# Router fed from raw rows, first gather begun with the first tile, x loaded first and later issues in a decoder layer's mixer

## The chip, the cores and the metric

The kernel runs on one core of a Trainium2 chip. The metric is device time in microseconds (us) of one execution. PE is TensorE, PEld its weight load, DVE is VectorE, ACT is ScalarE, POOL is GpSimd, SP is SyncE (here it only issues DMAs).

## What is computed

One layer of a decoder trunk on 256 tokens of width 1024, in fp32. Cut to what matters here:

```python
# 1 token mixer: one input projection feeds three causal mixers (gated DeltaNet, RG-LRU, window attention)
y = (g_a * y_a + g_b * y_b + g_c * y_c) @ w_out
x = LN1(alpha * x + y)                                   # gain ln1_g, offset ln1_b
# 2 channel mixer: top 4 of 32 experts
logits = x @ router_w + router_b
gates = softmax(top_k(logits, 4))
# each expert: clamped SwiGLU, 1024 -> 2 x 1024 -> 1024; its weights are 12.6 MB
x = LN2(alpha * x + sum_k gates[k] * expert[idx[k]](x))
# 3 per-layer embedding
x = LN3(alpha * x + sigmoid(x @ Wg) * (p @ Wp))
```

Nothing is dropped: every token reaches its four experts.

## The kernel before

**Mixer.** The weight matrices are cut into 117 pieces of 512 KB. `load` brings a piece on SP's queue into one of four buffers `w`; `split` makes of it a high part (ACT, L423) and a low part (DVE L426 and POOL L428), in a ring of three places, `HI` and `LO`; then PE multiplies (three products for each pair of parts, L367 and L377). `run` goes over the *units* (a unit is one piece's products, or some of them) by the index u: first the evacuation of the unit before, then loads and splits, then the unit's products, then one step of every *strand*. A strand is a generator (`evac_ab`, `decays`, `inverse`, `attend`, `bias_parts`, `router` and so on) that issues some instructions and gives way with `yield`; so one `yield` puts what follows behind another unit's products in the order of every engine. `events` says which strand may go on. Each engine works in the order of issue.

**End of the mixer.** The output projection is eight units (list at L1294). `out_unit` names (tile t of 128 tokens, half c of the columns, piece kp). Its first halves read the ring, its second halves read `xh`, `xl`, `RV` and `KT`. `evac` adds the residual into `xs` (L1153) and takes statistics; `first_norm` scales and shifts the rows on DVE (L1174, L1177), transposes them (L1186) and multiplies them with the router weights (L1192). `router` then works on tile 0 and tile 1 in turn, when both have been normalised: top four, softmax, and the seat of each token in each expert by a matmul with a triangle (L1223 to L1232).

**Experts.** `group` makes one-hot matrices of the seats (L1456) and gathers the tokens of two experts by matmul (`gathered`, L1448). `expert` multiplies with the up weights (L1485; 64 seats), applies SwiGLU, multiplies with the down weights (L1520); `spread` puts the result back to the tokens (L1545) and adds it into `Y` (L1556; the first one brings the residual, L1553). The weights come on SP's queue (L1375 up, L1387 down) into a ring of ten buffers of 2 MB: four (`F`) lie apart and are filled from the mixer on (`prefetch`, L1112), six (`wq`) lie where the mixer's tiles were. Such a buffer is loaded once the mixer's tiles under it have had their last use. One expert takes four buffers for up and two for down weights. The expert pools lie one behind the other in the order in which they are opened, and so do the mixer's.

Of the kernel before, what the change touches and what calls it, by code (L numbers as in the profile page):

```python
# [18 lines left out]
D = 1024  # L19
# [6 lines left out]
SLOTS = 64  # L26
NR = T // SLOTS - 1
# [56 lines left out]
class Routing:  # L84


    def __init__(self, pl):
# [6 lines left out]
        tail = pl.tile([P, 100], F32, name="tail")  # L94
        self.ex, self.sel, self.sm, self.counts = tail[:, 0:NE], tail[:, NE:2 * NE], tail[:, 64:66], tail[0:1, 68:68 + NE]

    def softmax(self, dve, t, ex, sel, sm):

        dve.tensor_tensor_reduce(out=ex, in0=ex, in1=sel, op0=ALU.mult, op1=ALU.add, scale=1.0, scalar=0.0, accum_out=sm)
        dve.reciprocal(sm, sm)  # L100
        dve.tensor_scalar(self.G[:, t], ex, sm, None, op0=ALU.mult)

# [9 lines left out]
def mixer(mx, tc, nc, a, xs, rt, dram, cst, ones, el):  # L112
# [80 lines left out]
    warm = mp.tile([P, 1], F32, name="warm")  # L193
    pool.memset(warm, 0.0)
# [6 lines left out]
    stB = m2.tile([65, P], F32, name="stB", tag="sq")  # L201
# [6 lines left out]
    def late_parameters():  # L208
# [11 lines left out]
        pool.dma_start(rw, a["router_w"][0].rearrange("(p k) e -> p k e", k=KD))  # L220
# [4 lines left out]
    def bias_parts():  # L225
# [20 lines left out]
    pool.memset(ones, 1.0)  # L246
# [7 lines left out]
    pr = mp.tile([P, 72], F32, name="pr")  # L254
# [21 lines left out]
    def softplus(dst, src, n, neg):  # L276
# [21 lines left out]
    def parameters():  # L298
        ps = yield from banks.take()
        pe.transpose(ps[:, :65], stB, ident[:65, :65])  # L300
        dve.tensor_copy(pr[:, :65], ps[:, :65])
# [276 lines left out]
    def evac_ab(ps):  # L578
# [19 lines left out]
        yield  # L598
        p2 = yield from banks.take()
# [59 lines left out]
    def decays():  # L659

        yield from wait("G")
        dts = []
# [45 lines left out]
    def inverse():  # L708
# [272 lines left out]
    def attend(gq, qT):  # L981
# [146 lines left out]

    def norm_rows():
        while cur[0] < S + 2:  # L1130
            yield
        M["gb"] = big("TG", [P, 2, D])
        for i, n in enumerate(("ln1_g", "ln1_b")):
            act.dma_start(M["gb"][:, i], a[n].to_broadcast([P, D]))
        M["xT"] = big("MG", [P, KD, T])

    out_ps = {}

    def out_unit(work, done):
# [10 lines left out]
        def evac(_):  # L1150
            for t, c in done:
                xv = xs[:, t, halves[c]]
                dve.scalar_tensor_tensor(xv, xv, 2.0 * ALPHA, out_ps[t, c], ALU.mult, ALU.add)  # L1153
                dve.bn_stats(lns[:, t, c], xv)
                if c == 0 and t == 0:
# [3 lines left out]
                    pool.memset(M["wk"][:, 0:80], -3.0e38)  # L1159
                if c:  # L1160
# [6 lines left out]

    def first_norm(t):

        xT, gb = M["xT"], M["gb"]  # L1170
        xc = wp.tile([P, KD * P], F32, name="xc", tag="w")
        for hf in range(2):
            c = slice(hf * 512, (hf + 1) * 512)
            dve.scalar_tensor_tensor(xc[:, c], xs[:, t, c], mv[:, t, 0:1], gb[:, 0, c], ALU.subtract, ALU.mult)  # L1174
        qk = lambda v, hf: v.rearrange("p (k q) -> p q k", q=KD)[:, 4 * hf:4 * hf + 4]
# [3 lines left out]
        if t == 0:  # L1179
            yield  # L1180
        else:
            events.add("n1")
        for hf in range(2):
            b = yield from banks.take()
            for k in range(4):
                pe.transpose(b[:, k * P:(k + 1) * P], xs[:, t, (4 * hf + k) * P:(4 * hf + k + 1) * P], ident)  # L1186
            act.copy(xT[:, 4 * hf:4 * hf + 4, t * P:(t + 1) * P], b.rearrange("p (k t) -> p k t", k=4))
            banks.done(b)
        if t == 0:
            yield  # L1190
        for k in range(KD):
            pe.matmul(M["rps", t][:, :NE], xT[:, k, t * P:(t + 1) * P], rw[:, k], start=k == 0, stop=k == KD - 1)  # L1192
        events.add(f"r{t}")

    def router():

        yield from wait("r0", "n1")
# [8 lines left out]
        ex, sel = (take(NE), rt.ex), (take(NE), rt.sel)  # L1206
        m8, m4, sm = two(take(16)), two(take(16)), (take(2), rt.sm)
        posm = rt.pos
        pool.memset(m4, -3.0e38)
        for t in range(2):  # L1210
            if t:
                yield from wait("r1")
            dve.tensor_add(lg[:, t, :NE], M["rps", t][:, :NE], rb)
# [7 lines left out]
            ps2 = yield from banks.take()  # L1221
            if t == 0:
                pe.matmul(ps2[:, :NE], stri, sel[0], start=True, stop=True)  # L1223
                rt.softmax(dve, 0, ex[0], sel[0], sm[0][:, 1:2])
            else:
                pe.matmul(ps2[:, :NE], ones, sel[0], start=True, stop=False)
                pe.matmul(ps2[:, :NE], stri, sel[1], start=False, stop=True)
                pe.matmul(ps2[0:1, NE:2 * NE], ones[:, 0:1], sel[0], start=True, stop=False)
                pe.matmul(ps2[0:1, NE:2 * NE], ones[:, 0:1], sel[1], start=False, stop=True)
                act.copy(rt.counts, ps2[0:1, NE:2 * NE])  # L1230
# [588 lines left out]
```

## Time and profile before

| | |
|---|---|
| median of 3 runs | 1422.58 us (1421.93 to 1425.25) |
| the profiled execution | 1420.59 us, its span 1418.8 us |
| busy | PE 95%, DVE 42%, ACT 26%, POOL 17% |
| DMA | 481.66 MB, mean 339 GB/s |

The span is the stretch that the trace covers; the execution's own time is 1.8 us longer. A busy PE is not PE at its peak, as matmuls overlap and their ends are modelled. Times in the rows are from the span's start. A releaser ("<-") is what ended the idle time in front of an instruction.

### The profile page before, as it was taken

The page shows a single profiled execution, that of the slowest core. Times are in us where ns is not written, and L with a number is a line of the kernel's source. Part 1 is how long each engine was busy: PE and PEld are TensorE (multiplying, and loading weights), DVE is VectorE, ACT ScalarE, POOL GpSimd, SP SyncE. Part 2 cuts the span into 40 slices and gives each one's busy share as a digit, 9 for nine tenths or more (in the row PEclk, how much of TensorE's full clock was granted, in tenths as well). Part 3 has the DMA queues.
Part 4 walks back from the last instruction along what each step waited for, and adds up shares of the span by engine and source line. Part 5 has one row for each costly group of instructions (what it writes and reads, how often), then busy time and mean ns, then how long its engine had stood idle before and what let it go on. Part 6 is the DMA issues. An engine that isn't in the chain of part 4 may idle for free. (4 is left out here: it accounts for less than half of the span.)

```text
span 1418.8 us, 19330 instructions
## 1 busy us (share of the span) xinstructions
PE 1343.1 (95%) x7720; PEld 748.0 (53%) x7721; DVE 591.8 (42%) x1245; ACT 372.4 (26%) x743; POOL 247.0 (17%) x217
## 2 busy tenths in 40 slices
PE   8999989999999999999999999999999999989987
PEld 7989967888887334334333333333333333333326
DVE  6398985865565133223222222222223222222238
ACT  6767464644551111111111110111111100111122
POOL 5554864434561000000000000000000000000000
PEclk9999999999998999999999999999999999999998
DMA  9755455345888999999999999999999999999970
GB/s 264 215 137 138 133 180 168 113 135 181 307 303 339 367 427 430 428 428 426 428 429 428 428 426 429 430 428 428 426 429 430 428 427 428 429 428 428 428 296 30
DMA packets 122133, 481.66 MB, mean 339 GB/s; under 512 B 11340, under 2 KB 69340, under 8 KB 88632
## 3 DMA queue, kind: packets, MB, share of 16 engines
q1 hardware_dynamic: 120440, 477.16, 84.4%
q0 software_dynamic: 848, 1.86, 0.4%
q10 hardware_dynamic: 752, 1.38, 0.3%
q8 instruction: 62, 1.02, 0.3%
q14 instruction: 31, 0.25, 0.0%
HBM read 478.78 MB, written 3.42 MB: 340 GB/s over the span
## 5 line engine op out<-in xcount | busy, mean ns | idle before, releaser
L1485 PE MATMUL gu<-w,xe 128*64 128x512 f32 x1168 | 262.9, 598 | 6.6 <-DMA w<-in_w_gu_dram 6.6
L1485 PE MATMUL gu<-F,xe 128*64 128x512 f32 x880 | 199.2, 596 | 4.8 <-DMA F<-in_w_gu_dram 4.8
L428 POOL TENSOR_TENSOR LO<-w,HI 128x384 fp32r<-128x384 f32 (+1 forms) x113 | 168.4, 1491 | 165.9 <-ACT HI L423 154.6
L1485 PEld LDWEIGHTS gu<-w,xe 128*64 128x64 f32 x1168 | 81.7, 137 | 164.8 <-issue 144.1
L426 DVE TENSOR_TENSOR LO<-w,HI 128x640 fp32r<-128x640 f32 (+1 forms) x113 | 117.1, 1038 | 83.5 <-ACT HI L423 81.8
L1503 DVE TENSOR_SCALAR gc<-gu 128x256 f32<-128x256 f32 x64 | 26.9, 421 | 266.9 <-PE gu L1485 266.9
L1416 POOL DMA_DIRECT2D pt<-in_p_dram x1 | 0.8, 777 | 789.2 <-DVE lc L1507 789.2
L423 ACT CAST HI<-w 128x1024 fp32r<-128x1024 f32 x113 | 118.0, 1044 | 59.2 <-PE pjt L377 36.6
L1520 PE MATMUL dn<-w,hT 128*64 128x512 f32 x560 | 130.0, 607 | 2.0 <-ACT hT L1513 2.0
L1556 DVE TENSOR_TENSOR Y<-Y,cb 128x512 f32<-128x512 f32 x124 | 79.5, 682 | 116.3 <-PE cb L1545 116.3
L367 PE MATMUL pjt<-xh,HI 128*128 128x256 f32 x424 | 124.7, 294 | 0.0
L1485 PEld LDWEIGHTS gu<-F,xe 128*64 128x64 f32 x880 | 60.2, 136 | 119.0 <-issue 104.9
L367 PE MATMUL pjt<-xh,LO 128*128 128x256 f32 x424 | 120.5, 284 | 1.3 <-DVE LO L426 1.3
L367 PE MATMUL pjt<-xl,HI 128*128 128x256 f32 x424 | 120.1, 283 | 0.0
L1520 PE MATMUL dn<-F,hT 128*64 128x512 f32 x464 | 106.0, 598 | 0.0
L1504 ACT ACTIVATE sg<-gc 128x256 f32<-128x256 f32 x64 | 26.8, 419 | 286.4 <-DVE gc L1503 286.4
L1448 PE MATMUL gat<-oh,xs 128*128 128x128 f32 x512 | 76.2, 294 | 24.7 <-DVE oh L1456 19.9
L1448 PEld LDWEIGHTS gat<-oh,xs 128*128 128x128 f32 x512 | 64.4, 197 | 44.4 <-issue 27.7
L367 PEld LDWEIGHTS pjt<-xh,HI 128*128 128x128 f32 x424 | 81.5, 192 | 1.8 <-issue 1.1
L367 PEld LDWEIGHTS pjt<-xh,LO 128*128 128x128 f32 x424 | 81.3, 192 | 2.0 <-DVE LO L426 1.9
L367 PEld LDWEIGHTS pjt<-xl,HI 128*128 128x128 f32 x424 | 81.5, 192 | 0.3
L1493 DVE TENSOR_TENSOR gt<-gwt,gt 128x256 fp32r<-128x256 f32 x32 | 13.6, 424 | 152.2 <-ACT gt L1492 152.2
(404 smaller groups left out, 1713.2 us busy)
## 6 DMA issues: line engine op xcount, KB each, us to landing
w<-in_w_gu_dram SPq DMA_DIRECT2D x73, 2048.0 KB, 29.2
F<-in_w_gu_dram SPq DMA_DIRECT2D x51, 2048.0 KB, 29.4
w<-in_w_down_dram SPq DMA_DIRECT2D x70, 1024.0 KB, 19.3
F<-in_w_down_dram SPq DMA_DIRECT2D x58, 1024.0 KB, 21.0
w<-in_w_in_dram SPq DMA_DIRECT2D x85, 512.0 KB, 3.8
F<-in_w_gu_dram SPq DMA_DIRECT2D x8, 1024.0 KB, 6.8
w<-in_w_o_lru_dram SPq DMA_DIRECT2D x8, 512.0 KB, 4.7
w<-in_w_o_swa_dram SPq DMA_DIRECT2D x8, 512.0 KB, 3.8
```

What stands on the lines that cost most here:

```text
L367: pe.matmul(ps, hl[l][:, k * P:(k + 1) * P], b[r][:, k], start=k == 0 and n == 0, stop=k == KD - 1 and n == 2)
L423: act.copy(hi, s)
L426: dve.tensor_sub(lo[:, 0:n], s[:, 0:n], hi[:, 0:n].bitcast(F32))
L428: pool.tensor_tensor(out=lo[:, n:], in0=s[:, n:], in1=hi[:, n:].bitcast(F32), op=ALU.subtract)
L1416: pool.dma_start(pt, a["p"][0, 0].rearrange("(t p) c -> p t c", p=P))
L1448: pe.matmul(ps[:, kk], xs[:, t, k * P:(k + 1) * P], oh[:, t], start=t == 0, stop=t == 1)
L1485: pe.matmul(gu[64 * j:64 * j + 64, b], xe[:, k], w[:, j * D + b * 512:j * D + (b + 1) * 512], start=False, stop=k == KD - 1)
L1493: dve.tensor_sub(gt[:, 1], ps, gt[:, 0].bitcast(F32))
L1503: dve.tensor_scalar(gc[:, c], guv[:, c, 0], 7.0, None, op0=ALU.min)
L1504: act.activation(sg[:, c], gc[:, c], AF.Sigmoid, scale=1.702)
L1520: pe.matmul(dn[64 * jj:64 * jj + 64], hT[:, 2 * hf + kk, j * 64:j * 64 + 64], w[:, kk, jj * 512:(jj + 1) * 512], start=hf == j == kk == 0, ...
L1556: dve.tensor_add(y, y, pss[jj])
```

## The change

- **Order and place.** x is loaded ahead of the first weight piece, and twelve matmuls on a tile of ones run first; the first `split` comes behind the transposes of x. `evac_ab` and `decays` give way once more ahead of their matmuls, `inverse` twice more ahead of its transpose, `softplus` twice less. The `b_gu` rows are loaded on SP's queue. The attention rows are normalised on ACT.
- **Router.** Its weights are scaled by the gain beforehand (`router_weights`), and the mean's and the offset's parts are added behind (`lc_`). So the rows are transposed as they come out of the output projection, half by half (`logits`). ACT scales the rows into `xs` without gain and offset; these are applied when the gather is evacuated (`scaled_rows`) and in a separate pass for the residual (`residual`, which loads the layer-norm rows on ACT's queue).
- **Order at the end.** The output units finish tile 0 first. The router takes tile 0 by itself; its one-hot matrix and its half of the first gather come ahead of tile 1's.

```diff
+        self.oh = pl.tile([P, 2, GRP * SLOTS], F32, name="oh1")
+        self.gb = pl.tile([P, 2, KD], F32, name="gb1")
...
+    def places(self, dve, iota, t, e):
+        dve.tensor_tensor(out=self.oh[:, t].rearrange("p (e s) -> p e s", e=GRP), in0=iota[:, :SLOTS].unsqueeze(1).to_broadcast([P, GRP, SLOTS]),
+                          in1=self.pos[:, t, e:e + GRP].unsqueeze(2).to_broadcast([P, GRP, SLOTS]), op=ALU.is_equal)
+    def second(self, dve, act, pe, ps, ones, stri):
+        pe.matmul(ps[:, :NE], ones, self.sel0, start=True, stop=False)
+        pe.matmul(ps[:, :NE], stri, self.sel, start=False, stop=True)
...
+        self.seat(dve, 1, ps[:, :NE], self.sel)
+        act.copy(self.counts, ps[0:1, NE:2 * NE])
...
-                pool.dma_start(raw_b[32 * n:32 * n + 32], bsrc[g_])
+                sync.dma_start(raw_b[32 * n:32 * n + 32], bsrc[g_])
...
-            if c in (13, 9, 5):
+            if c == 9:
                 yield
...
             dve.scalar_tensor_tensor(g[:, t], g[:, t], -1.0, alog, ALU.mult, ALU.mult)
+        yield
         yield
...
         yield from wait("G")
+        yield
...
             sync.dma_start(T0[16 * b:16 * b + 16, :, c], td[b].rearrange("s i c -> i s c"))
         yield
         yield
+        yield
+        yield
...
-            dve.tensor_scalar(pr3[:, hh, 0:P], pr3[:, hh, 0:P], sm[:, 0, hh:hh + 1], None, op0=ALU.mult)
-            dve.tensor_scalar(pr3[:, hh, P:384], pr3[:, hh, P:384], sm[:, 1, hh:hh + 1], None, op0=ALU.mult)
+            act.mul(pr3[:, hh, 0:P], pr3[:, hh, 0:P], sm[:, 0, hh:hh + 1])
+            act.mul(pr3[:, hh, P:384], pr3[:, hh, P:384], sm[:, 1, hh:hh + 1])
...
+    lc_ = mpa.tile([P, 2, NE], F32, name="lc1")
...
+                if t not in rows:
+                    rows[t] = wp.tile([P, KD * P], F32, name="y", tag="w")
+                y = rows[t][:, halves[c]]
+                dve.scalar_tensor_tensor(y, xs[:, t, halves[c]], 2.0 * ALPHA, out_ps[t, c], ALU.mult, ALU.add)
...
+    def logits(t, c):
+        xT = M["xT"]
+        b = yield from banks.take()
+        for k in range(4):
+            pe.transpose(b[:, k * P:(k + 1) * P], rows[t][:, (4 * c + k) * P:(4 * c + k + 1) * P], ident)
+        act.copy(xT[:, 4 * c:4 * c + 4, t * P:(t + 1) * P], b.rearrange("p (k t) -> p k t", k=4))
+        banks.done(b)
+        yield
+        for k in range(4 * c, 4 * c + 4):
+            pe.matmul(M["rps", t][:, :NE], xT[:, k, t * P:(t + 1) * P], rw[:, k], start=k == 0, stop=k == KD - 1)
...
     def first_norm(t):
-        for hf in range(2):
-            dve.scalar_tensor_tensor(xc[:, c], xs[:, t, c], mv[:, t, 0:1], gb[:, 0, c], ALU.subtract, ALU.mult)
-        for hf in range(2):
-            dve.scalar_tensor_tensor(xs[:, t, 512 * hf:512 * hf + 512].rearrange("p (q k) -> p q k", q=4), qk(xc, hf),
-                                     mv[:, t, 2:3], qk(gb[:, 1], hf), ALU.mult, ALU.add)
+        yield
+        dve.scalar_tensor_tensor(mv[:, t, 3:4], mv[:, t, 0:1], -1.0, mv[:, t, 2:3], ALU.mult, ALU.mult)
+        for hf in range(2):
+            act.activation(xs[:, t, 512 * hf:512 * hf + 512].rearrange("p (q k) -> p q k", q=4), y[:, 4 * hf:4 * hf + 4],
+                           AF.Identity, scale=mv[:, t, 2:3], bias=mv[:, t, 3:4])
...
-    for work, done in ((both(0), ()), (both(1), ()), (second(0, 0, 1), ()), (both(2), ()), (both(3), ((0, 0), (1, 0))),
-                       (second(0, 2, 3), ((0, 1),)), (second(1, 0, 1), ()), (second(1, 2, 3), ((1, 1),))):
+    for work, done in ((both(0), ()), (both(1), ()), (second(0, 0, 1), ()), (first(0, 2, 3), ((0, 0),)),
+                       (second(0, 2, 3), ((0, 1),)), (first(1, 2, 3), ((1, 0),)), (second(1, 0, 1), ()), (second(1, 2), ()),
+                       (second(1, 3), ((1, 1),))):
...
-    load(0)
     for i in range(4):
         sync.dma_start(xs[:, :, i * 256:(i + 1) * 256], xsrc[:, :, i * 256:(i + 1) * 256])
+    load(0)
+    ps = bank(4)()
+    for _ in range(12):
+        pe.matmul(ps[:, 0:P], ones, ones, start=True, stop=True)
...
-    split(order[0][0])
     for _ in transpose_x():
         pass
+    split(order[0][0])
...
+    def scaled_rows(xe, k2, ps):
+        for kk in range(2):
+            k = 2 * k2 + kk
+            act.activation(xe[:, k], ps[:, kk], AF.Identity, scale=rt.gb[:, 0, k:k + 1], bias=rt.gb[:, 1, k:k + 1])
...
+        pss = [p1.tile([P, 2, GRP * SLOTS], F32, name="gat", tag="cb", bufs=3) for _ in range(3)]
+        pss.append(p1.tile([P, 2, GRP * SLOTS], F32, name="gat", tag="ms"))
+        for t in range(2):
+            if t:
+                rt.second(dve, act, pe, p1.tile([P, 2 * NE], F32, name="seats", tag="tr"), ones, stri)
+                rt.places(dve, iota, 1, 0)
+            for k in range(KD):
+                pe.matmul(pss[k // 2][:, k % 2], xs[:, t, k * P:(k + 1) * P], rt.oh[:, t], start=t == k % 2 == 0, stop=t == k % 2 == 1)
+                if t and k % 2:
+                    scaled_rows(xe, k // 2, pss[k // 2])
+                    yield
...
+    def residual():
+        g1, b1 = (w2.tile([P, D], F32, name=n, tag=n, bufs=1) for n in ("ob", "bd"))
+        for v, n in ((g1, "ln1_g"), (b1, "ln1_b")):
+            act.dma_start(v, a[n].to_broadcast([P, D]))
...
```

## Rows read from the trace of the kernel before

**Rows 1.** Windows: length; PE, PEld, DVE, ACT, POOL busy (instructions); PE's clock; DMA share; GB/s.
```profile
500.00:1360.00 860.00, 825.39 (x4068) 320.70 (x4065) 229.28 (x516) 100.70 (x251) 0.78 (x1) 1.00 1.01 428
```

**Rows 2.** Waits of PE, 1200 to 1370 us: total us, times, longest.
```profile
PE gu L1485 <- DMA w<-in_w_gu_dram: 4.3, 5, 1.2
```

**Rows 3.** Timeline of SP's queue: start us, us, what it issues, count.
```profile
418.57 1.85 SPq L1387 DMA_DIRECT2D w<-in_w_down_dram  x4
432.25 0.33 SPq L1375 DMA_DIRECT2D w<-in_w_gu_dram  x1
440.41 1.28 SPq L1375 DMA_DIRECT2D w<-in_w_gu_dram  x3
461.98 0.80 SPq L1387 DMA_DIRECT2D F<-in_w_down_dram  x2
```

**Rows 4.** Windows around the handover from mixer to experts.
```profile
438.00:441.00 3.00, 3.00 (x18) 2.44 (x17) 2.91 (x4) 0.19 (x1) 0.00 (x0) 1.00 0.26 109
447.00:456.00 9.00, 7.52 (x36) 6.96 (x37) 4.50 (x29) 1.41 (x5) 0.56 (x1) 0.50 1.00 430
457.00:463.00 6.00, 6.00 (x36) 2.96 (x34) 0.00 (x0) 0.74 (x2) 0.00 (x0) 1.00 0.10 14
483.00:486.00 3.00, 2.54 (x13) 0.80 (x10) 0.00 (x0) 0.37 (x1) 0.00 (x0) 1.00 0.54 137
```

**Rows 5.** Timeline of PE at the handover: start us, us, instruction, count, idle before.
```profile
417.36 0.39 PE L377 MATMUL pjt<-HI,AT 128*128 128x512 f32 x1
...
431.78 0.39 PE L377 MATMUL pjt<-LO,AT 128*128 128x512 f32 x1
...
440.17 1.14 PE L1186 MATMUL pg<-cst,xs 128*128 128x128 f32 x8
...
441.57 1.08 PE L1192 MATMUL pg<-rw,MG 128*128 128x32 f32 x8
...
453.20 3.91 PE L1448 MATMUL gat<-oh,xs 128*128 128x128 f32 x16 [0.35 <-DVE oh L1456]
457.04 1.94 PE L1485 MATMUL gu<-F,xe 128*64 128x512 f32 x8
```

**Rows 6.** Timeline of PE in the mixer, where it stood idle.
```profile
106.06 0.39 PE L600 MATMUL pg<-sc,F 128*128 128x16 f32 x2 [1.70 <-DVE sc L597]
...
112.15 2.07 PE L671 MATMUL pg<-cst,gcc 128*128 128x128 f32 x8 [1.96 <-ACT gcc L604]
121.25 1.14 PE L671 MATMUL pg<-cst,gcc 128*128 128x128 f32 x8
...
189.81 0.50 PE L377 MATMUL pjt<-LO,xh 128*128 128x512 f32 x1 [1.81 <-POOL LO L428]
...
204.19 0.50 PE L377 MATMUL pjt<-LO,xh 128*128 128x512 f32 x1 [1.47 <-DVE LO L426]
```

**Rows 7.** Timeline of POOL and of ACT around 188 us.
```profile
187.12 1.58 POOL L234 DMA_DIRECT2D rawb<-in_b_gu_dram  x3
...
190.32 0.62 ACT L240 CAST bias<-rawb 96x512 bf16<-96x512 f32 x1 [5.75 <-DMA rawb<-in_b_gu_dram]
```

**Rows 8.** Timeline of PE at the start.
```profile
5.62 1.09 PE L271 MATMUL pg<-cst,xs 128*128 128x128 f32 x4 [5.62 <-DMA xs<-in_x_dram]
...
9.79 0.36 PE L367 MATMUL pjt<-xh,HI 128*128 128x256 f32 x1
...
10.11 0.28 PE L367 MATMUL pjt<-xh,LO 128*128 128x256 f32 x1
10.23 0.28 PE L367 MATMUL pjt<-xh,HI 128*128 128x256 f32 x1
```

**Rows 9.** Groups of ACT by line: shape, count, busy us, mean ns, idle before.
```profile
L1018 ACT ACTIVATE F<-F,st 128x256 f32<-128x256 f32 x16 | 7.9, 494 | 0.0
...
L1017 ACT ACTIVATE F<-F,st 128x128 f32<-128x128 f32 x16 | 6.3, 396 | 0.1
```

**Rows 10.** Timeline of DVE at the handover.
```profile
443.72 2.21 DVE L1177 SCALAR_TENSOR_TENSOR xs<-xc,mv,TG 128x512 f32<-128x512 f32 x2
```

More of the change, by code (lines that the diff above doesn't have):

```diff
@@ L26 @@
 SLOTS = 64
+GRP = 2
 NR = T // SLOTS - 1
@@ L1127, in held_piece, with router_weights @@
         return dst
+    lc_ = mpa.tile([P, 2, NE], F32, name="lc1")
+    def router_weights():
+        yield from wait("late", "att3")
+        col = lambda i: pr[:, 65 + 8 * i:73 + 8 * i].unsqueeze(2).to_broadcast([P, KD, NE])
+        rb_ = m2.tile([P, T], F32, name="rwb", tag="sq").rearrange("p (k e) -> p k e", e=NE)
+        sums_ = m2.tile([P, T], F32, name="rws", tag="sq").rearrange("p (n e) -> p n e", e=NE)
+        dve.tensor_tensor(out=rb_, in0=rw, in1=col(1), op=ALU.mult)
+        dve.tensor_reduce(out=sums_[:, 1], in_=rb_.rearrange("p k e -> p e k"), axis=AX.X, op=ALU.add)
+        yield
+        dve.tensor_tensor(out=rw, in0=rw, in1=col(0), op=ALU.mult)
+        dve.tensor_reduce(out=sums_[:, 0], in_=rw.rearrange("p k e -> p e k"), axis=AX.X, op=ALU.add)
+        yield
+        ps = yield from banks.take()
+        pe.matmul(ps[:, 0:2 * NE], ones, sums_[:, 0:2].rearrange("p n e -> p (n e)"), start=True, stop=True)
+        yield
+        dve.tensor_scalar(lc_[:, 0], ps[:, 0:NE], -1.0, None, op0=ALU.mult)
+        dve.tensor_add(lc_[:, 1], ps[:, NE:2 * NE], rb)
+        banks.done(ps)
     def norm_rows():
@@ L1166, in out_unit @@
         return products, evac, ()
+    def logits(t, c):
[5 more added lines that the diff above has]
+        banks.done(b)
+        yield
+        for k in range(4 * c, 4 * c + 4):
+            pe.matmul(M["rps", t][:, :NE], xT[:, k, t * P:(t + 1) * P], rw[:, k], start=k == 0, stop=k == KD - 1)
+        if c:
+            events.add(f"r{t}")
     def first_norm(t):
-        xT, gb = M["xT"], M["gb"]
-        xc = wp.tile([P, KD * P], F32, name="xc", tag="w")
+        yield
+        dve.scalar_tensor_tensor(mv[:, t, 3:4], mv[:, t, 0:1], -1.0, mv[:, t, 2:3], ALU.mult, ALU.mult)
+        y = rows[t].rearrange("p (k q) -> p q k", q=KD)
         for hf in range(2):
-            c = slice(hf * 512, (hf + 1) * 512)
-            dve.scalar_tensor_tensor(xc[:, c], xs[:, t, c], mv[:, t, 0:1], gb[:, 0, c], ALU.subtract, ALU.mult)
-        qk = lambda v, hf: v.rearrange("p (k q) -> p q k", q=KD)[:, 4 * hf:4 * hf + 4]
-        for hf in range(2):
-            dve.scalar_tensor_tensor(xs[:, t, 512 * hf:512 * hf + 512].rearrange("p (q k) -> p q k", q=4), qk(xc, hf),
-                                     mv[:, t, 2:3], qk(gb[:, 1], hf), ALU.mult, ALU.add)
[L1179 to L1182, printed above, removed]
-        for hf in range(2):
[L1184 to L1193, printed above, removed]
+            act.activation(xs[:, t, 512 * hf:512 * hf + 512].rearrange("p (q k) -> p q k", q=4), y[:, 4 * hf:4 * hf + 4],
+                           AF.Identity, scale=mv[:, t, 2:3], bias=mv[:, t, 3:4])
+        events.add(f"n{t}")
     def router():
-        yield from wait("r0", "n1")
+        yield from wait("r0", "n0")
         wk = M["wk"]
@@ L1220, in router @@
             act.activation(ex[t], lg[:, t, :NE], AF.Exp, bias=sm[t][:, 0:1])
-            ps2 = yield from banks.take()
             if t == 0:
+                rt.softmax(dve, 0, ex[0], sel[0], sm[0][:, 1:2])
+                yield
+                ps2 = yield from banks.take()
                 pe.matmul(ps2[:, :NE], stri, sel[0], start=True, stop=True)
[L1224 to L1230, printed above, removed]
-            dve.scalar_tensor_tensor(posm[:, t], ps2[:, :NE], 1.0, sel[t], ALU.add, ALU.mult)
-            dve.tensor_scalar(posm[:, t], posm[:, t], -1.0, None, op0=ALU.add)
-            banks.done(ps2)
+                yield
+                rt.seat(dve, 0, ps2[:, :NE], sel[0])
+                banks.done(ps2)
+                rt.places(dve, iota, 0, 0)
     def note(name, f):
@@ L1448, in gathered @@
                     pe.matmul(ps[:, kk], xs[:, t, k * P:(k + 1) * P], oh[:, t], start=t == 0, stop=t == 1)
-            act.copy(xe[:, 2 * k2:2 * k2 + 2], ps)
+            scaled_rows(xe, k2, ps)
             yield
     def group(e):
-        oh = w2.tile([P, 2, GRP, SLOTS], F32, name="oh1", tag="oh1", bufs=1)
-        for t in range(2):
-            dve.tensor_tensor(out=oh[:, t], in0=iota[:, :SLOTS].unsqueeze(1).to_broadcast([P, GRP, SLOTS]),
-                              in1=posm[:, t, e:e + GRP].unsqueeze(2).to_broadcast([P, GRP, SLOTS]), op=ALU.is_equal)
@@ L1609, in moe @@
     gu, first = begun(0), gather
-    next(first)
-    rt.finish(dve)
+    rest = residual()
+    next(rest)
     for _ in range(2):
         next(first)
+    rt.finish(dve)
     for e in range(NE):
@@ L1621, in mid @@
                 next(first, None)
+                if k in (3, 5, 7):
+                    next(rest, None)
             if e == BIASED:
```

87 lines of the change are left out of this document (49 added, 38 removed).

## The prediction

> **What bounds the kernel now.** I read the windows first. They show two stages. From 500 us on the DMA engines are full, at 428 GB/s, to the end of the weights [rows 1]. The waits view says who feels it: in the last experts PE's products stop for `w_gu` [rows 2]; ahead of 1000 us no product does. So PE starts the experts with ten buffers filled and is caught up by the stream; after that, the end is the end of the stream plus a tail that the change does not touch. The question in the expert stage is therefore not when the first expert starts, but how many microseconds the DMA engines stand idle ahead of 500 us. The queue's own timeline [rows 3] and the windows around the handover [rows 4] answer it: idle 0.74 x 3 = 2.2 us around 440, where the queue waits for the last output products to free weight buffers; 0.90 x 6 = 5.4 us around 460, where all ten buffers are full and the first expert has freed none; 0.46 x 3 = 1.4 us around 484. In all 9.0 us.
>
> Ahead of that, in the mixer, PE is the bound, and everything later (the prefetch too, which hangs on the strands' events) moves with it. There I looked for stalls in PE's timeline [rows 6].
>
> **The mixer, part by part.** *Yields.* The cumulative sums of the decay (L600) and the broadcasts (L671) were issued in the round in which their input is made: PE stood 1.70 and 1.96 us, and the eight L671 matmuls after the stall took 2.07 us where the next eight took 1.14 [rows 6]. The change puts a round between each pair and shortens softplus by two rounds. A round is a unit of products, about 2.9 us there (24 matmuls 0.12 us apart, as soon as they run freely [rows 8]), more than either stall. So 1.70 + 1.96 + 0.93 = 4.6 us come back; at worst the stall reappears behind another late input, which makes it 0. The two yields ahead of `inverse`'s transpose free DVE, not PE: 0.
>
> *The `b_gu` rows on SP's queue instead of POOL's.* At 187.12 POOL spends 1.58 us issuing three loads, ahead of the low halves that PE waits 1.81 us for [rows 6, 7]. ACT meanwhile stands 5.75 us for the same rows and casts nothing [rows 7], since POOL issued them behind memsets. SP would issue them as soon as its last weight load is out. I count the 1.81 us, and about 1.2 us of the next stall (1.47 us [rows 6]), in which DVE is late with a low half behind attention normalisation that now goes to ACT: 3.0 us in all, between 0 and 3.3. The Trainium skill ("DMA: Bandwidth & Descriptors", Issuing engines are not separate DMA queues) says that another issuing engine saves only sequencer time; by it the move is worth at most the 1.58 us on POOL, and the sum would be 1.4 us smaller. The row of ACT is against taking it alone here, because it is the issue's place in POOL's order that is late, not the transfer.
>
> *Normalisation of the attention rows on ACT.* 32 multiplications leave DVE. The nearest rows on ACT cost 0.40 us for 128 columns and 0.49 for 256 [rows 9]: 4 x (0.40 + 0.49) = 3.6 us for each of four calls, 14.2 us. ACT has waits to hide that in; I count 0, and take it up as a rival.
>
> *x first, and twelve warming matmuls.* PE's first work waits for x until 5.62 us, its first product starts at 9.79 [rows 8]. x is now issued ahead of the first weight, which brings it perhaps 1.5 us sooner. But the warming matmuls stand in front of the transposes: 24 records at the slow clock's 3.91/16 = 0.24 us each [rows 5] are up to 5.9 us from about 1.1 us on, so the transposes start between 5 and 7; and the cast of the first weight now stands behind the four casts of x. I count a loss of 0.5 us, between a gain of 1.5 and a loss of 1.5.
>
> Mixer: 4.6 + 3.0 - 0.5 = 7.1 us sooner.
>
> **The handover.** All times here are on the old clock, without the 7.1 us. Output products run from 417.36; each (tile, half, piece) is six matmuls, 1.37 us, 16 of them up to 440.40 [rows 5]. New order: tile 0 complete first, then tile 1. Between them now stand three rounds of transposes and router products on the unnormalised rows: four router matmuls (8 records) 1.0 us [rows 5], four transposes about 0.5 (eight took 1.14 [rows 5]), so 3 x 1.5 = 4.5 us. The last use of the HI/LO ring (tile 1, first half, piece 3) ended at 431.78 + 0.39 [rows 5]; two more products (2.7 us) and one set of transposes (0.5) now stand ahead of it, so about 435.4. The last product moves to 440.4 + 4.5 = 444.9.
>
> Which buffers wait for what? Expert 0's down weights go to buffers 5 and 4, expert 1's up weights to 3, 2, 1, 0, in that order and in order on SP. Before, 5 and 4 were free at once (four issues at 418.57), 3 came free with the ring (432.25), the others with the last products (440.41) [rows 3]. By the tile sizes the mixer's tiles move up by 128 + 1024 + 64 bytes (routing tiles) and another 256 (`lc1`), 1472; the expert buffers by 1216 - 1024 = 192, as the one-hot leaves `w2`. Buffer 4 began 960 bytes behind `LO`; now it begins 320 bytes inside it. So its load waits for the ring, as buffer 3's does, and everything behind it on SP waits too.
>
> The stream then: buffer 5's 2 MB and the last 0.5 MB of output weights, from about 420 on, are through at about 426.2 (an estimate, at 428 GB/s); the next issue is at 435.5, and data flow at about 436.4 (an idle queue took some 0.9 us to restart around 440.41 and 461.98). Idle 10.2 us. From there 10 MB for buffers 4 to 0 (24.5 us; the issue at 444.9 comes in time, and buffer 1, which now lies over `lc1`, waits for the router at about 448, also in time) and the 1 MB of layer-norm rows, which moves from the mixer to ACT's queue behind the router (2.4 us, the same bytes as before): busy to 463.3.
>
> *Router and first gather.* By then the first expert must have freed a buffer. Before, that took from 440.40 to 461.98 [rows 3, 5], of it 16.6 us to the first expert product at 457.04. With the last product 4.5 us later, the old chain would give 466.5. Removed from it: DVE's scale and shift (2.21 us, 443.72 [rows 10]) and the subtraction ahead of them, since the raw rows are transposed as they land; half of the first gather (of 3.91 us [rows 5]), begun with tile 0; and PE has work there, so its clock should not fall to 0.50, its 1.2 GHz level, as from 447 on [rows 4]. I put the first expert product at 451 to 453, the first free buffer at 454 to 457: well ahead of 463.3, so the gap at 460 is gone, and the one at 484 too. But that is all it buys: 10.2 us of idle in place of 9.0, a loss of 1.2.
>
> *In the experts* the gather's copy becomes two scaled activations: 2 x 0.40 us [rows 9] in place of one instruction, at most 0.4 to 0.8 us more on PE's chain for each; while PE is ahead of the stream and later waits for it, that costs nothing. The residual's extra passes are on DVE, idle more than half of the time [rows 1]. Without that cover the 64 gather steps would cost 26 us or more.
>
> Sum: 1420.6 (the profiled execution's own time) - 7.1 + 1.2 = 1414.7. The median shown is 2.0 us above that execution, so 1416.7 beside it.
>
> **The rivals.**
> *Deeper gain:* buffer 4 is not held (the overlap is not there, or only touched bytes count). Then 4 MB flow to about 430.9 and the idle time is 5.5 us: 3.5 us less than before in place of 1.2 more, 1412.0. For it: buffers 5 and 4 were free together before. Against: the sizes. Chance 0.20.
> *No change:* the yields only move the stalls, or DVE, ACT and POOL bound the rounds; the mixer gains 0 to 2.5 us. 1421.3 to 1423.8. For it: in-order engines with many small strands; the stall at 204.19 came 14 us behind the one at 189.81 [rows 6]. Chance 0.23.
> *Slower:* the 14.2 us of multiplications stand on ACT ahead of the casts that PE waits for; if all reach PE, 14.2 - 7.1 + 1.2 = 8.3 us slower, 1430.9. It decides slower from about 10.2 us reaching PE on. Against it: at 190.32 ACT stood idle for 5.75 us [rows 7]. Chance 0.07. The Trainium skill ("ScalarE: Activation LUTs", Rules for kernel authors) says to keep multiplications on VectorE and off ScalarE, which speaks for this rival; the rows here show the two engines close in fp32.
>
> **How the numbers follow.** The forecast has 0.50, with its own range 1413 to 1420. 0.3% of 1422.6 is 4.3 us, about what a measurement of this kernel can tell from no change, so faster means under 1418.3: three quarters of the forecast (0.38) and the deeper gain (0.20), 0.58. Same: the rest of the forecast (0.12) and the no-change case (0.23), 0.35. Slower 0.07. The range that leaves out no more than 2 in 10 takes in the deeper gain with 2 us below it and most of the no-change case: 1410 to 1422.5.
>
> **What would show it.** L600 and L671 without idle time; POOL without L234's issues, ACT without the 5.75 us wait. First product later than 9.79. In the queue's timeline two down issues at once and two held up to the ring's last product; DMA idle some 10 us ahead of that, and none around 460 and 484. First expert product some 4 us sooner than the mixer's shift explains, worth nothing. The prediction is wrong if all four down issues still come together, if PE stalls elsewhere in the mixer for the sum saved, or if the stream is no longer full behind 500 us.

## The result, and the profile after

The changed kernel takes 1439.81 us (median of 4, 1438.55 to 1441.27) beside 1422.26 for the kernel before: a ratio of 1.0129, 95% interval 1.0113 to 1.0145. It is 17.5 us slower; 1416.7 was forecast, with 1410 to 1422.5 as the range. The profiled execution took 1440.74, its span 1438.9, 20.1 us more than before.

Where the 20.1 us lie is read from SP's queue. The first issue of a down weight, which the mixer's end sets, moved from 418.57 [rows 3] to 432.69: 14.1 us are lost in the mixer of this execution. From there to the end it was 1418.8 - 418.57 = 1000.2 us and is now 1006.2: another 6.0. First the expert stage, the same window as [rows 1], same columns:

```profile
500.00:1360.00 860.00, 820.14 (x3992) 320.91 (x3990) 222.60 (x507) 123.07 (x307) 0.78 (x1) 0.98 1.01 425
```

The DMA engines are as busy as before (1.01), but move 425 GB/s where they moved 428. The prediction took this rate for given. SP's timeline and the windows at the handover, after:

```profile
432.69 17.52 SPq L1438 DMA_DIRECT2D w<-in_w_down_dram  x4
450.31 24.82 SPq L1426 DMA_DIRECT2D w<-in_w_gu_dram  x4
476.09 1.81 SPq L1438 DMA_DIRECT2D F<-in_w_down_dram  x4
```

```profile
441.00:444.00 3.00, 3.00 (x15) 2.47 (x14) 2.07 (x3) 1.23 (x2) 1.70 (x2) 1.00 0.08 33
444.00:447.00 3.00, 3.00 (x17) 2.51 (x16) 1.63 (x4) 0.39 (x1) 0.06 (x1) 1.00 0.00 0
447.00:450.00 3.00, 3.00 (x20) 2.58 (x18) 1.51 (x4) 0.20 (x1) 0.60 (x2) 1.00 0.00 0
450.00:453.00 3.00, 3.00 (x18) 2.54 (x18) 0.88 (x3) 2.35 (x3) 0.00 (x0) 1.00 0.80 279
474.00:477.00 3.00, 3.00 (x17) 1.01 (x14) 2.44 (x4) 1.13 (x1) 0.00 (x0) 1.00 0.47 123
483.00:486.00 3.00, 1.36 (x10) 1.20 (x10) 2.34 (x7) 0.62 (x3) 0.00 (x0) 1.00 1.01 427
```

Up to 465 us this is the handover as forecast: the four down issues last 17.52 us, because two are held up to the ring's last product, and the DMA engines are idle for 9 to 10 us ahead of 450. One gap that was to go is still there: from 468 to 477 the engines are idle for 2.4 us (the line of 474 is the worst of it). By then the first expert had freed a buffer (its products on the first one end at 470.55), but the next load into it is issued only at 476.09: SP works in order, and the issue ahead of it, at 474.81, had waited (total us, times, longest) for the layer-norm rows that the change loads on ACT's queue from 463.83 on:

```profile
SPq L1426 <- DMA ob<-in_ln_g_dram: 12.3, 1, 12.3
```

In the built program both loads report to the same completion semaphore, so the later one waits for the earlier; every other profile of a kernel with the new router has this wait too (11.6 to 12.3 us). No run takes it away, so its price is not shown. Summed over 36 windows of 2.5 us from the first down issue, the engines stood idle 11.1 us before and 13.1 after. PE is at 1.00 of 2.4 GHz here, where it was at 0.50 [rows 4], and the first expert product comes at 466.10, 33.4 us behind the first down issue in place of 38.5 [rows 3, 5].

The mixer is another matter. Some signs are as forecast: the products that were L600 and L671 (now L627 and L699) start without idle time, and ACT's wait for the bias rows is 3.72 us in place of 5.75 [rows 7]. The first product starts at 10.05 in place of 9.79 [rows 8]. But PE's largest total of waits from 60 to 300 us (total us, times, longest) is now one that was small. Before and after:

```profile
PE pjt L377 <- ACT TG L536: 0.5, 1, 0.5
```

```profile
PE pjt L403 <- ACT TG L562: 7.5, 2, 4.3
```

PE's timeline, ACT's (with the wait for the bias rows on top) and DVE's at the second of the two times:

```profile
217.82 0.79 PE L403 MATMUL pjt<-HI,F 128*128 128x512 f32 x1 [4.34 <-ACT TG L562]
```

```profile
193.68 0.62 ACT L267 CAST bias<-rawb 96x512 bf16<-96x512 f32 x1 [3.72 <-DMA rawb<-in_b_gu_dram]
...
212.76 1.03 ACT L449 CAST HI<-w 128x1024 fp32r<-128x1024 f32 x1
215.80 0.40 ACT L1055 ACTIVATE F<-F,st 128x128 f32<-128x128 f32 x1 [2.00 <-DVE st L1053]
216.11 0.49 ACT L1056 ACTIVATE F<-F,st 128x256 f32<-128x256 f32 x1
216.51 0.38 ACT L1055 ACTIVATE F<-F,st 128x128 f32<-128x128 f32 x1
216.80 0.49 ACT L1056 ACTIVATE F<-F,st 128x256 f32<-128x256 f32 x1
217.20 1.05 ACT L562 ACTIVATE TG<-pjt 128x512 f32<-128x512 f32 x2
```

```profile
214.57 0.96 DVE L1052 TENSOR_TENSOR st<-st 128x8 f32<-128x8 f32 x1
215.56 0.20 DVE L1053 RECIPROCAL st<-st 128x8 f32<-128x8 f32 x1
```

The gate's evacuation (L562) copies PE's finished products out and so frees the place for the next ones. It stands in ACT's queue behind four of the new multiplications (L1055, L1056), and these wait for a reciprocal on DVE that is issued in the same round. PE stands 4.34 us; ACT's 2.00 us of waiting and 1.4 us of these multiplications lie in that time. The groups of ACT from 150 to 300 us give the work of the 32 multiplications, 6.3 + 7.9 = 14.2 us as forecast from [rows 9], and what stood ahead of them:

```profile
L1056 ACT ACTIVATE F<-F,st 128x256 f32<-128x256 f32 x16 | 7.9, 496 | 0.0
...
L1055 ACT ACTIVATE F<-F,st 128x128 f32<-128x128 f32 x16 | 6.3, 394 | 5.5 <-DVE st L1053 5.4
```

A second place, at 38 us, is of another kind: a DVE instruction on 8 columns that took 4.05 us where the shortest of its kind takes 0.16, and POOL's timeline beside it:

```profile
31.04 4.05 DVE L317 SCALAR_TENSOR_TENSOR spe<-spe,spq 128x8 f32<-128x8 f32 x1
```

```profile
29.62 0.97 POOL L245 DMA_DIRECT2D rw<-in_router_w_dram  x1
30.59 0.55 POOL L247 DMA_DIRECT2D gb<-in_ln_g_dram  x1
31.14 0.54 POOL L247 DMA_DIRECT2D gb<-in_ln_b_dram  x1
31.69 0.75 POOL L525 TENSOR_TENSOR RV<-RV,AT 128x256 f32<-128x256 f32 x1
32.39 1.03 POOL L454 TENSOR_TENSOR LO<-w,HI 128x384 fp32r<-128x384 f32 x1
33.37 0.74 POOL L525 TENSOR_TENSOR RV<-RV,AT 128x256 f32<-128x256 f32 x1
34.06 1.00 POOL L454 TENSOR_TENSOR LO<-w,HI 128x384 fp32r<-128x384 f32 x1
35.01 0.72 POOL L525 TENSOR_TENSOR RV<-RV,AT 128x256 f32<-128x256 f32 x1
```

The instruction ends at 35.09, when the POOL instruction of 34.06 ends (35.06), though the next one stands right behind it. After it DVE's convolutions are late, and PE waits 3.07 us at 37.54. The cast of the weight's high part on ACT that stood at 46.98 in the kernel before comes at 53.95, 6.97 us late; so half of the 14.1 us lie ahead of 55 us in this execution:

```profile
46.98 1.04 ACT L423 CAST HI<-w 128x1024 fp32r<-128x1024 f32 x1
```

```profile
53.95 1.04 ACT L449 CAST HI<-w 128x1024 fp32r<-128x1024 f32 x1
```

### The profile page after: what moved, and what is told of

Its sections match the earlier page's. It is cut to its first block, busy times and chain, and to the rows that moved or that the text cites. A ratio compares the mean times of both kernels' runs of the same rounds, so it can differ in the third digit from the quotient of the medians.

```text
span 1438.9 us, 19433 instructions
## 1 busy us (share of the span) xinstructions
PE 1352.8 (94%) x7746; PEld 755.0 (52%) x7747; DVE 587.6 (41%) x1223; ACT 413.9 (29%) x843; POOL 243.6 (17%) x207
## 5 line engine op out<-in xcount | busy, mean ns | idle before, releaser
L454 POOL TENSOR_TENSOR LO<-w,HI 128x384 fp32r<-128x384 f32 (+1 forms) x113 | 171.4, 1518 | 186.0 <-ACT HI L449 175.8
L1501 PE MATMUL gat<-oh,xs 128*128 128x128 f32 x480 | 72.2, 296 | 37.5 <-DVE oh L110 19.5
L1501 PEld LDWEIGHTS gat<-oh,xs 128*128 128x128 f32 x480 | 60.8, 199 | 55.2 <-issue 26.0
L1604 PEld LDWEIGHTS dn<-w,hT 128*64 128x64 f32 x560 | 37.3, 138 | 71.6 <-issue 60.9
```

Of the source, the lines that this page charges most:

```text
L454: pool.tensor_tensor(out=lo[:, n:], in0=s[:, n:], in1=hi[:, n:].bitcast(F32), op=ALU.subtract)
L1501: pe.matmul(ps[:, kk], xs[:, t, k * P:(k + 1) * P], oh[:, t], start=t == 0, stop=t == 1)
L1604: pe.matmul(dn[64 * jj:64 * jj + 64], hT[:, 2 * hf + kk, j * 64:j * 64 + 64], w[:, kk, jj * 512:(jj + 1) * 512], start=hf == j == kk == 0, ...
```

## The experiments

Times are medians, in us; the kernel before ran beside each set (1421.2 to 1422.0). Single executions of one kernel spread by 2 to 9 us (ten of the changed and aligned kernel of experiment 3 lie between 1419.2 and 1424.6), and a profile shows one of them, so differences of 2 to 3 us between two profiles are not proof by themselves. The run of experiment 1 is called run 1. Three theories stood against each other for the mixer: the multiplications on ACT, the small DVE instructions held up by POOL, and the new start. For the stream: where the buffers lie.

**1. Normalisation back on DVE** (all else as changed).

```
-            act.mul(pr3[:, hh, 0:P], pr3[:, hh, 0:P], sm[:, 0, hh:hh + 1])
+            dve.tensor_scalar(pr3[:, hh, 0:P], pr3[:, hh, 0:P], sm[:, 0, hh:hh + 1], None, op0=ALU.mult)
...
```

> The changed kernel with the normalisation of the attention rows back on DVE; all else as changed. Theory (multiplications on ACT): the two stalls of PE behind ACT's gate evacuation, 3.13 us at 200 and 4.34 us at 218, and the slow clock behind them go, some 8 us faster than the changed kernel, about 1432. Rival (DVE is late instead, or these stalls hang on the exponentials, which wait for DVE's small row operations in either form): 0 to 2 us, 1438 to 1440.

1432.55 (ratio to before 1.0086, 1.0059 to 1.0112): 7.3 faster than the changed kernel. Of PE's two stalls behind the gate's evacuation, that of 4.34 is gone, and the other, 3.13 in the changed kernel, stays:

```profile
PE pjt L403 <- ACT TG L562: 3.1, 1, 3.1
```

The first down issue is at 423.19, 9.5 us ahead of the changed kernel's. Not all of this is the multiplications: the cast at 53.95 stands at 50.53 here, 3.4 us sooner, and up to there the two kernels are the same. Behind it the two executions differ by 6.1.

**2. Where the multiplications' price comes from.** One round between the reciprocal and the multiplications; and the multiplications alone in the kernel before.

```
         dve.reciprocal(sm, sm)
+        yield
         for hh in range(4):
             act.mul(...)
...
         yield
-        yield
         PT = yield from PTs.take()
```

> The changed kernel with one round between DVE's reciprocal and the multiplications on ACT (and one fewer behind them). Theory (head of the line: ACT stands 1.96 and 2.00 us at 203 and 214 for the reciprocal, with the gate evacuation and the casts that PE wants queued behind it): most of the stalls of 3.13 and 4.34 us go, 4 to 6 us faster than the changed kernel, about 1435. Rival (ACT is simply full, 14.2 us of work ahead of casts): 0 to 1.5 us.

> The kernel before with nothing changed but the 32 multiplications of the attention rows on ACT. Theory (they are dear by themselves, 14.2 us of ACT work of which about half reaches PE): 6 to 8 us slower, 1428 to 1430. Rival (they are dear only together with the bias rows on SP's queue and the new rounds): 0 to 2 us slower.

With the round: 1431.88 (1.0075), 7.9 faster than the changed kernel, all of the price, with the same 14.2 us of multiplications on ACT. ACT's waits for the reciprocal, 5.4 us in the changed kernel, are gone, and PE's waits from 180 to 225 us hold one for the gate where there were two:

```profile
PE pjt L403 <- ACT TG L562: 3.4, 1, 3.4
```

Alone in the kernel before, without the round: 1431.35 (1.0080, 1.0051 to 1.0109), 9.4 slower, with waits of ACT for the reciprocal of 2.42 and 2.00 us (1.96 and 2.00 in the changed kernel) and 4.33 us of PE behind the gate's evacuation:

```profile
PE pjt L377 <- ACT TG L536: 6.5, 2, 4.3
```

So the multiplications are not dear as work, but by where they stand in an in-order queue. The round moves two things at once: ACT no longer waits for the reciprocal, and the four multiplications no longer stand right ahead of the gate's evacuation. How the price splits between the two (2.0 and 1.4 us of ACT's time at the stall shown) no run separates.

**3. Where the weight buffers lie.** In the program's memory map the four F buffers begin at 20480 before, a multiple of 512, and at 21696 after, 192 behind one; the six w buffers at 129440 (416 behind one) and at 129632 (96 behind one). Unused bytes shift them: in the kernel before 192 bytes ahead of F (the changed kernel's places), 256 bytes ahead of F, or 96 ahead of w (all ten at multiples of 512); and in run 1's kernel 320 ahead of F and 96 ahead of w (all ten again). The edits of the first and the third:

```
     rt = Routing(pp)
+    pp.tile([P, 48], F32, name="pad")
...
+    wq.tile([P, 24], F32, name="pad2", tag="pad2")
     for i in range(RING - EARLY):
         held(i, [P, 4096])
```

> The kernel before with 192 unused bytes ahead of everything that the change moves up by 192: the weight buffers then begin exactly where those of the changed kernel do with respect to 512 bytes (F 192, w 96 behind a multiple); nothing else is changed. Theory (where the buffers begin): 425 GB/s in the expert stage, and 940 us at 428 become 946.6, so 6 to 7 us slower, about 1428. Rival: 428 GB/s and no change.

> The kernel before with 96 unused bytes ahead of its six w buffers, so that all ten weight buffers begin at multiples of 512 bytes; before, the four F buffers did and the six w buffers began 416 bytes behind one. Theory (the stream's rate hangs on where the buffers begin): more than 428 GB/s in the expert stage, 430 or more, and so 4 to 10 us faster, 1412 to 1418. Rival (where they begin is nothing to the stream, and the 425 GB/s of the changed kernel has another cause): 428 GB/s and the same time.

> The kernel before with 256 unused bytes ahead of the F buffers: these begin 256 bytes behind a multiple of 512, the w buffers 160. Theory (what counts is a multiple of 256): 428 GB/s in the expert stage and no change, 1421 to 1422. Rival (what counts is a multiple of 512 or more): 425 to 426 GB/s, 3 to 5 us slower.

> The changed kernel with the normalisation on DVE, and with unused bytes (320 ahead of the F buffers, 96 ahead of the w buffers) so that all ten begin at multiples of 512 bytes. Against the run with the normalisation on DVE alone, 1432.6. Theory (where the buffers begin): 430 GB/s or more, 8 to 14 us faster, 1419 to 1424. Rival (PE is close to the bound there by the longer gathers, or the scaled copies cost the stream): 0 to 3 us faster.

The windows from 500 to 800 us of these four, in the same order (shifted by 192; aligned; shifted by 256; changed and aligned):

```profile
500.00:800.00 300.00, 292.08 (x1472) 115.88 (x1470) 82.96 (x186) 34.56 (x88) 0.00 (x0) 1.00 1.01 425
```

```profile
500.00:800.00 300.00, 292.09 (x1472) 115.78 (x1470) 82.99 (x186) 34.55 (x88) 0.00 (x0) 1.00 1.01 429
```

```profile
500.00:800.00 300.00, 292.08 (x1472) 115.90 (x1470) 82.99 (x186) 34.57 (x88) 0.00 (x0) 1.00 1.01 428
```

```profile
500.00:800.00 300.00, 287.22 (x1440) 114.69 (x1440) 81.52 (x186) 43.37 (x110) 0.00 (x0) 0.99 1.01 428
```

Times: 1426.01 (1.0031, 1.0014 to 1.0048), 4.8 slower; 1417.72 (0.9976, 0.9959 to 0.9993), 3.5 faster; 1421.26 (0.9998), the same; 1421.10, 11.5 faster than run 1. In these windows the engines' work is equal to the instruction in the first three; only the places differ. The places of the changed kernel make its 425 GB/s, and 256 bytes off is as good as none. The Trainium skill ("DMA: Bandwidth & Descriptors", How a descriptor splits into AXI transactions) says that a descriptor, one contiguous stretch of a transfer, is cut at multiples of 256 bytes, and that one which starts between them spends time on bytes that it doesn't use. It tells this of bytes that are fetched; what moved here is the place written in SBUF. The four runs agree on the 256 bytes; they do not show the mechanism.

**4. The first 50 us.** Of the changed kernel: the first softplus's two rounds given back; the columns' loads from SP. Of run 1's kernel: the columns' and the router's loads from SP; the old start.

```
-            if c == 9:
+            if c == 9 or neg and c in (13, 5):
...
-            pool.dma_start(rt.gb[:, i], ...)
+            sync.dma_start(rt.gb[:, i], ...)
...
-        pool.dma_start(rw, ...)
+        sync.dma_start(rw, ...)
```

> The changed kernel with the two rounds given back inside the first softplus (that of the lambda parameters) alone; the second softplus stays short. Theory (the trimmed softplus queues more small two-input DVE instructions in one round, and one of them was held for 4.05 us behind POOL's work): the stall of 3.07 us at 37.5 and the slow clock behind it go, 5 to 7 us faster, about 1434. Rival (POOL's new column loads put POOL behind, and its instructions then stand back to back and hold DVE in any case): under 2 us.

> The changed kernel with the two loads of the layer norm's columns issued from SP's queue and not from POOL's. Theory (POOL's loads put POOL behind, so its instructions stand back to back and hold DVE's small ones): the 4.05 us instruction falls under 1 us and 5 to 7 us come back, about 1434. Rival (the trimmed softplus alone does it): under 2 us.

> The changed kernel with the normalisation on DVE (1432.6), and with the router's weights and the two loads of columns issued by SP in place of POOL. Theory (POOL's late loads put its instructions back to back, and a small DVE instruction of two SBUF inputs is then held 2.4 to 4 us): none of these instructions over 1 us, the ladder at the twelfth cast at +1.2 in place of +3.5, 2 us faster, about 1430.5. Rival (they are held anyway): no change.

> The changed kernel with the normalisation on DVE and with the old start: the first weight's load ahead of x, its split ahead of the transposes, no warming products. Against 1432.6. Theory (the new start is 3 to 4 us dearer and not 0.5, because the first cast of the weight comes at 9.1 us in place of 4.7): 3 to 4 us faster, about 1429. Rival (the ladder's 3.5 us are given back later, or came from elsewhere): 0 to 1 us.

The softplus: 1439.62, nothing. Its profile shows the 4.05 us instruction again (at 30.91), so the shorter softplus is not what makes it; yet PE waits only 1.67 us there, and the cast that stood at 46.98 comes 3.19 us late in place of 6.97. In the profiles of three runs whose kernels are the same up to there (run 1, the added round of experiment 2, the bias rows on POOL of experiment 5) it comes 2.95 to 3.67 late. So 6.97 is what one execution shows; how often the changed kernel has it is open. The columns alone: 1438.92, within the spread; an instruction of 2.77 us starts while the router's load is being issued (30.31). With the router's load gone from POOL too: 1428.75 (1.0045, 1.0028 to 1.0062), 3.8 faster than run 1 by the medians, though the two intervals just meet and the profiled executions are 1.9 us apart at the first down issue (421.31 and 423.19). Its DVE timeline has at that place two of these instructions in 1.63 us:

```profile
31.08 1.63 DVE L317 SCALAR_TENSOR_TENSOR spe<-spe,spq 128x8 f32<-128x8 f32 x2
```

In run 1 the longest was 2.40 us, and the cast came 3.55 us late; here it comes 1.23 late. The old start: 1432.28, nothing (0.3, within the spread), so the theory that the new start is dear is refuted as well.

**5. The bias rows and the decay's rounds.** The changed kernel with the bias rows on POOL again; the kernel before with the rounds of the decay alone (and the second softplus two rounds shorter); the aligned kernel before with both, and with the rounds alone.

```
-                pool.dma_start(raw_b[32 * n:32 * n + 32], bsrc[g_])
+                sync.dma_start(raw_b[32 * n:32 * n + 32], bsrc[g_])
...
         yield from wait("G")
+        yield
         dts = []
```

> The changed kernel with the rows of the up-projection's bias loaded from POOL's queue again. Theory (as predicted, the move to SP is worth about 3 us): 3 us slower, 1443. Rival (SP's queue is in order, the loads there wait behind weight loads and hold ACT's casts, or the bias rows come at a worse time): 0 to 4 us faster.

> The kernel before with the rounds of the decay alone: one more round ahead of the cumulative sums and one ahead of the broadcasts, and the second softplus shorter by two. Prediction's term: PE's stalls of 1.70 and 1.96 us go and 0.93 us of slow products with them, 4.6 us faster, about 1416.6. Rival (the stalls go, but most of the time is given back in the next 40 us, as the ladder of the changed kernel shows, some 1.7 us net): 1419.5.

> The kernel before with all weight buffers at multiples of 512 bytes (1417.7), the rounds of the decay, and the rows of the up-projection's bias on SP's queue; nothing of the start, the normalisation, the handover or the router. If the terms add, 1417.7 less 1.7 and less 3.2: about 1412.8, and faster than both kernels. Rival (in-order engines give the gains back one to the other): 1415 to 1417.

> The kernel before with all weight buffers at multiples of 512 bytes and the rounds of the decay, the bias rows left on POOL's queue. If the terms add, 1421.2 less 3.5 and less 1.0: about 1416.7, the fastest so far. Rival (the bias rows on SP were what made the earlier sum 1416.9): 1418 to 1419.

Bias rows back on POOL: 1442.99 (1.0151, 1.0130 to 1.0173), 3.2 slower by the medians, as forecast; from the cast that stood at 46.98 to the first down issue the two profiled executions differ by 2.9. The rounds alone: 1420.86 (0.9993, 0.9984 to 1.0003), 1.1 faster in place of 4.6, and not clear of the spread. The stalls at L600 and L671 are gone, but the waits of PE from 60 to 300 us, from 10.2 us before (without the one for "issue", which stands in both), come to 9.4: it waits more often for low halves, and 2.1 us for the gate in place of 0.5.

```profile
PE pjt L377 <- POOL LO L428: 2.3, 1, 2.3
PE pjt L377 <- ACT TG L536: 2.1, 1, 2.1
PE pjt L367 <- DVE LO L426: 1.9, 4, 0.6
PE pjt L377 <- DVE cv L462: 1.4, 1, 1.4
PE pjt L367 <- POOL LO L428: 1.0, 1, 1.0
PE pg L639 <- ACT sq L635: 0.7, 1, 0.7
```

Rounds and bias rows on the aligned kernel: 1416.90 (0.9968, 0.9955 to 0.9980), where 1412.8 was hoped for; rounds alone 1418.55 (0.9977). Without the multiplications the bias rows on SP are thus worth 1.3 by the ratios, and the intervals overlap. ACT's timeline of the former shows where the time may go:

```profile
187.24 0.62 ACT L240 CAST bias<-rawb 96x512 bf16<-96x512 f32 x1 [2.65 <-DMA rawb<-in_b_gu_dram]
...
193.86 0.21 ACT L1017 ACTIVATE st<-st 128x8 f32<-128x8 f32 x1 [3.29 <-DVE st L1015]
```

The wait of 5.75 us [rows 7] is now 2.65, but 6 us later ACT stands 3.29 us for DVE, and PE's wait for the gate is 3.9 us, 2.1 in the kernel with the rounds alone.

**6. The handover, and the inverse.** On the changed, aligned kernel with DVE's normalisation (1421.1): the w buffers another 512 bytes up, so that buffer 4 leaves the LO ring; and without the two rounds ahead of the inverse's transpose.

> The changed kernel with the normalisation on DVE and all weight buffers at multiples of 512 bytes (1421.1), with the six w buffers another 512 bytes further up, so that buffer 4 begins 288 bytes behind the LO ring and no longer inside it. Prediction's rule (a load waits for whatever its buffer overlaps): four down issues come together at about 421, the DMA engines stand idle 4 to 5 us less ahead of 500, and the time falls by as much, to about 1416.5. Rival (those 2 MB only move the idle time behind, to where the buffers are full): two issues at once are seen, but the time stays within 1 us.

> The changed kernel with the normalisation on DVE and all weight buffers at multiples of 512 bytes (1421.1), and without the two new rounds ahead of the inverse's transpose. Prediction's term: the two rounds are worth nothing to PE, no change. Rival (the later inverse shifts small products to where the engines are late, and the 1.7 us that the mixer loses between 221 and 247 come from there): 1 to 2 us faster.

Without the inverse's rounds: 1421.32, nothing, as forecast. Buffer 4 free: 1420.83, nothing, though SP's timeline shows four down issues at once:

```profile
422.56 2.15 SPq L1440 DMA_DIRECT2D w<-in_w_down_dram  x4
439.39 25.31 SPq L1428 DMA_DIRECT2D w<-in_w_gu_dram  x4
```

```profile
432.00:435.00 3.00, 3.00 (x14) 2.46 (x14) 2.21 (x3) 0.18 (x1) 1.77 (x2) 1.00 1.03 434
435.00:438.00 3.00, 3.00 (x17) 2.46 (x16) 1.74 (x4) 0.59 (x1) 0.00 (x0) 1.00 0.15 63
...
444.00:447.00 3.00, 3.00 (x21) 2.70 (x21) 1.99 (x12) 0.91 (x2) 0.00 (x0) 1.00 0.59 251
447.00:450.00 3.00, 2.36 (x16) 1.69 (x14) 1.57 (x3) 0.20 (x1) 0.00 (x0) 1.00 0.34 79
```

The 2 MB flow earlier, and the idle time moves behind them, to 436 and to 445 to 450, where the next buffers wait for the last products (12.0 us in place of 13.0 in all). The overlap that the prediction worked out was real, and worth no more than the spread (1420.83 and 1421.10).

**7. The change mended:** DVE's normalisation, aligned buffers, the router's loads on SP.

> The changed kernel with the normalisation on DVE, all weight buffers at multiples of 512 bytes, and the router's weights and columns issued by SP. If the terms add, 1421.1 less 3.8: about 1417.3, as fast as the aligned kernel before, so that the new handover and router are worth nothing. Rival (the 3.8 us hung on a state of the start that these addresses do not meet, as the twelfth cast came at +1.2 already there): 1420 to 1421.

1420.67 (0.9993, 0.9983 to 1.0003): as fast as without the router's move (1421.1), 2 to 3 slower than the aligned kernel before (1417.72, 0.9976), though the intervals overlap. With these buffer places and the router's load still on POOL (the last kernel of experiment 3), this load already came 2.6 us sooner than in run 1 (27.02 in place of 29.66), and none of the small DVE instructions took over 0.91 us. So what the router's loads cost seems to hang on when they fall; why they fall sooner at these places is open.

## Why the prediction was wrong

The medians chain from the kernel before to the changed one (the kernel before came out at 1421.2 to 1422.3 in the sets, so a link is good to one or two microseconds): 1421.2, with the buffers' places 1426.0 (+4.8), with start, rounds, bias rows on SP, handover and router, and the router's loads off POOL 1428.75 (+2.7), on POOL 1432.55 (+3.8), with the multiplications on ACT 1439.8 (+7.3).

*The step that failed most: normalisation on ACT "I count 0".* The 14.2 us of work were right to the tenth. The premise was wrong that what counts is whether ACT has idle time for them: they cost 7.3 us (9.4 alone in the kernel before), and nothing one round later. The rival "slower" had the sign and was right that the work stands ahead of what PE waits for, but not that its amount sets the price: with a round between, the same work costs nothing. What stands behind the multiplications in ACT's queue, and what they wait for, was not asked. The Trainium skill ("ScalarE: Activation LUTs", Rules for kernel authors), which spoke for that rival, compares costs per element; by the run with the round (1431.88, beside 1432.55 on DVE) these were not what decided.

*"The question in the expert stage is ... how many microseconds the DMA engines stand idle ahead of 500 us."* It left out the rate. The prediction itself worked out that the expert buffers move by 192 bytes, and asked only what they overlap. What 860 us move at 428 GB/s takes 866.1 at 425, 6.1 more; the buffers' places alone, in the kernel before, cost 4.8.

*Yields, 4.6:* measured 1.1, within the spread of nothing. The stalls went; the rival's sentence that "the yields only move the stalls" is what happened.

*`b_gu` rows, 3.0:* measured 3.2 in the changed kernel and 0 to 1.3 without the multiplications. The Trainium skill ("DMA: Bandwidth & Descriptors", Issuing engines are not separate DMA queues) gives only the sequencer's time as the gain, 1.58 us by the row of POOL; the first measurement lies above it, but with four runs on each side not clear of it, and the second doesn't decide.

*Start, -0.5:* measured -0.3, within the spread. Not forecast at all: the router's loads on POOL, 2 to 4 where they fall late.

*Handover, -1.2:* 2.0 us more idle time (13.1 for 11.1) where 1.2 were forecast; from the first down issue to the end the changed kernel takes 1.8 us more than the shifted kernel before (1006.2 and 1004.4), run 1's kernel 3.0. The held issues, the idle time ahead of 450 and the first expert product (33.4 us behind the first down issue) were right. Wrong was the step "so the gap at 460 is gone": the layer-norm rows were counted as 2.4 us of bytes, and not as something that SP's next load waits for, 12.3 us, while the freed buffer stood empty from 470.55 to 476.09. The rival "deeper gain" is refuted by experiment 6. How the 2.7 us split between handover, start, rounds and bias rows is not settled to the microsecond.

## What to carry to other kernels

An instruction that is moved to another in-order engine takes its wait along: look at what stands behind it there, and put a round between it and its input. The same holds for a queue of loads: ask of each new load which later one will wait for it. After any change of a tile's size, look where the buffers of a saturated stream begin; 192 bytes cost 4.8 us here, and 96 unused bytes gave the kernel before 3.5 us, more than any single part of the change did. A stall removed where many strands share in-order engines is a gain only if the sum of the waits falls, so price it by that and not by its own length.

## What the hardware showed unexpectedly

A small DVE instruction with two SBUF inputs can be held while POOL works, and for longer than one POOL instruction: in seven of the profiles one that takes 0.16 us otherwise took 2.36 to 4.05, while POOL's stood back to back. It ended when a POOL instruction ended (35.09 and 35.06 in the changed kernel, 33.45 and 33.42 in run 1, in both with a further one right behind); what lets it through at that one and not before is open. The Trainium skill ("SBUF — State Buffer", Who interferes with whom) says that of two such instructions the later one blocks until the other's ends; the trace agrees on the blocking, and shows in addition that it can last over several instructions. The stream's rate depends on the buffers' first byte: 425, 428 and 429 GB/s for 192 and 96, 0 and 416, 0 and 0 bytes behind a multiple of 512 (F and w buffers).
